# A four-layer decoder trunk: the order of the out projection's blocks, the place of two transposes, and the banks of the last product

## The chip, the core and the metric

The kernel runs on one core of a Trainium2 chip. The core has a matrix engine (TensorE, "PE" in the profile; "PEld" is its weight load), a vector engine (VectorE, "DVE"), a scalar engine (ScalarE, "ACT"), a general engine (GpSimd, "POOL") and a queue engine that issues most transfers (SyncE, "SP"). Each engine executes its own instructions in order, and an instruction that waits holds up everything behind it on that engine. The metric is the device time of one execution in microseconds; lower is better. The time before is the median of three runs, 1155.24 us (1154.94 to 1155.57).

## What is computed

The reference is a decoder trunk of four layers over 256 tokens of width 1024, in float32. Each layer is a token mixer and a squared-ReLU MLP, each behind an RMS norm, on one residual stream:

```
for i in range(4):
    a = rms_norm(h, attn_norm_g[i])
    y = mixer[i % 3](a)            # 0 differential attention, 1 MoBA, 2 sliding window
    h = h + y                      # y ends with  o @ w_out
    b = rms_norm(h, mlp_norm_g[i])
    h = h + square(max(b @ w_up[i], 0)) @ w_down[i]
return rms_norm(h, final_norm_g)
```

So layers 0 and 3 use differential attention (8 heads, each the difference of two attentions of width 64, with a normalized result of width 128), layer 1 MoBA and layer 2 sliding-window attention. The width of the MLP is 4096.

## The kernel before

All products are made from split operands: a float32 matrix is taken as a high part that fits the fast matmul format and a low part, and a product is the sum of high by high, high by low and low by high. `mm3` (L271 to L273) issues the three as matmuls of their own; `block_step` (L599, L600) joins two of them into one matmul of 512 columns.

The weights arrive in 185 pieces of 128 x 2048 (1 MB each) through SyncE's queue (L66) into four buffers called raw. `stage` splits each piece in two halves of 1024 columns: ScalarE copies the high part (whi, L80), VectorE subtracts it from the raw one to get the low part (wlo, L81). whi and wlo have three buffers each (LOOK + 1). `take` fetches and stages pieces ahead of their use, so a new piece goes into the buffer of the piece three places before it, and its copy waits until TensorE has read that one for the last time.

The residual stream is kept transposed, as four tiles hT0 to hT3 of 128 x 512; each holds two blocks d of 128 rows by 256 tokens (d = 0 to 7, block d in tile d // 2, half d % 2). `into` (L611 to L621) takes a finished product of block d out of its PSUM bank: VectorE adds it to hT (L618), then `norm_part` makes the operand of the next product, hg: its high part on ScalarE (L228), its low part on VectorE (L229). After the second block of a tile `norm_sum` squares it on ScalarE (L233) and adds up on VectorE (L238).

`out_proj_all` is the out projection of layers 0, 2 and 3. Its four weight pieces are four groups g of 256 of its 1024 inputs. In each g it goes over the eight blocks d; two blocks share a PSUM bank (p_d0 to p_d3), each block takes six matmuls in a g (two inputs of `mm3`), and in the last g each block goes to `into` when it is done. The MLP's `up_proj` follows (p_up, banks of another pool), whose first group goes over the eight blocks of hg in their order. Layer 1 has `out_proj`, which is not touched.

The mixer of layers 0 and 3 makes six projections in turn (`proj`, p_in: two of queries and keys, one of values, and the same again) and works on the heads in between. The list `plan` says which step of which head stands midway of each projection (even entries) or after it (odd ones): QK splits queries and keys, SC makes scores, TR transposes the weights, AV multiplies by the values and normalizes, OUT transposes the normalized result of a pair of heads (o, L404) on TensorE (p_o, L409) and splits it into the operand oo (L411, L412).

The last MLP product of layer 3 is `down_out`: two column halves c of 512 by two row halves t of 128 tokens, each in a bank p_last; res holds the residual stream in rows. `close` (L698) adds a finished bank to res on VectorE and squares it on ScalarE (L700); `finish` (L706 to L719) makes the reciprocal root and writes the rows out. For the last bank (c = 1, t = 1) the last weight piece is taken by halves of 256 columns, so that the first half is closed while the second is multiplied.

At the start WARM matmuls of a tile of ones (p_warm, L133) run while the first input arrives; each is executed as two passes.

What order the instructions have on each engine is not the source's alone: a scheduler that builds the program places them by its own estimate of times, within the dependencies. Dependencies through PSUM are kept by bank: a matmul into one half of a bank waits for a read of the other half.

## Time and profile before

| | before |
|---|---|
| median of three runs | 1155.24 us |
| lowest and highest | 1154.94, 1155.57 us |
| the profiled execution's own time | 1155.61 us |
| its span, first to last instruction | 1153.7 us |
| TensorE busy | 1140.0 us (99% of the span) |
| VectorE busy | 824.2 us (71%) |
| ScalarE busy | 672.1 us (58%) |
| mean granted TensorE clock | 0.998 of full |
| mean rate of the transfers | 172 GB/s |

The page of the profile shows one execution. A row of its timeline begins with the start and the duration in us, then the engine, the line of the kernel, the operation, the tiles as out<-in and the shape; a bracket gives the idle time of the engine before it and what ended that. Matmuls are pipelined, so one may show 0.28 us where the next starts 0.12 us later: the step from start to start is what counts. The chain that ended last is followed back from the last instruction to what released each step.

### The profile page before, as it was taken

What the parts mean: (1) busy time and instruction counts of PE and PEld (TensorE: products, weight loads), DVE (VectorE), ACT (ScalarE), POOL (GpSimd) and SP (SyncE); (2) the same over time, 40 slices, a digit from 0 to 9 for tenths busy, and PEclk for the clock granted to TensorE, in tenths of its full rate; (3) what the DMA queues carried; (4) which work ended last, traced back from release to release, by engine and by line L of the source; (5) the groups of instructions that cost most, each with busy time, mean ns of one, the idle gap of its engine ahead of it and who ended that gap; (6) DMA issues with size and microseconds to landing.
All of it is one profiled execution on the core that took longest, in us unless ns stands there. A gap on an engine that the chain in (4) does not pass through costs nothing.

```text
span 1153.7 us, 17107 instructions
## 1 busy us (share of the span) xinstructions
PE 1140.0 (99%) x6558; PEld 987.4 (86%) x6558; DVE 824.2 (71%) x1631; ACT 672.1 (58%) x1239; POOL 11.5 (1%) x39
## 2 busy tenths in 40 slices
PE   9999999999999999999999999999999999999997
PEld 7788888888887888888899888888888889888886
DVE  7987877656666698776568787775567787777453
ACT  6876655544476765654447866654447676665342
POOL 1000000000000000000000000000000000000000
PEclk9999999999999999999999999999999999999999
DMA  8543455555543355555564245555553444554551
GB/s 320 201 139 118 157 208 187 195 202 182 183 146 135 121 182 187 199 198 182 183 211 141 76 147 200 201 183 183 186 199 131 151 148 145 191 201 166 186 179 36
DMA packets 30608, 198.66 MB, mean 172 GB/s; under 512 B 3520, under 2 KB 5184, under 8 KB 7360
## 3 DMA queue, kind: packets, MB, share of 16 engines
q1 hardware_dynamic: 30240, 197.06, 49.5%
q8 instruction: 51, 0.84, 0.3%
q10 hardware_dynamic: 288, 0.52, 0.1%
q14 instruction: 29, 0.24, 0.1%
HBM read 196.52 MB, written 1.05 MB: 171 GB/s over the span
## 4 chain that ended last, share of the span: by engine, by line
PE 92%; DVE 5%; DMA 1%; ACT 1%; issue 1%; SPq 0%; DVEq 0%; ACTq 0%
PE p_up L599 20%; PE p_in L296 16%; PE p_down L599 15%; PE p_up L600 11%; PE p_down L600 8%; PE p_last L271 2%; PE p_last L273 2%; PE p_last L272 2%; DVE wlo L81 2%; PE p_t L351 1%; PE p_d L273 1%; PE p_d L271 1%; PE p_d L272 1%; PE p_av L434 1%; PE p_s L271 1%; DMA raw<-in_weights 1%
## 5 line engine op out<-in xcount | busy, mean ns | idle before, releaser
L81 DVE TENSOR_TENSOR wlo<-raw,whi 128x1024 fp32r<-128x1024 f32 (+1 forms) x374 | 447.2, 1210 | 202.0 <-ACT whi L80 201.3
L80 ACT ACTIVATE whi<-raw 128x1024 fp32r<-128x1024 f32 (+1 forms) x374 | 384.7, 1046 | 207.4 <-issue 111.0
L599 PE MATMUL p_up<-hg,whi 128*128 128x512 f32 x1024 | 356.8, 393 | 0.5 <-DVE hg L229 0.2
L600 PE MATMUL p_up<-hg,wlo 128*128 128x256 f32 x1024 | 285.5, 280 | 0.0
L599 PE MATMUL p_down<-uu,whi 128*128 128x512 f32 x768 | 266.4, 391 | 0.0
L599 PEld LDWEIGHTS p_up<-hg,whi 128*128 128x128 f32 x1024 | 191.4, 187 | 42.7 <-DVE hg L229 0.7
L600 PE MATMUL p_down<-uu,wlo 128*128 128x256 f32 x768 | 215.0, 280 | 0.0
L296 PE MATMUL p_in<-whi,hg 128*128 128x512 f32 (+1 forms) x736 | 213.2, 372 | 0.2 <-ACT whi L80 0.2
L600 PEld LDWEIGHTS p_up<-hg,wlo 128*128 128x128 f32 x1024 | 193.5, 189 | 0.5
L599 PEld LDWEIGHTS p_down<-uu,whi 128*128 128x128 f32 x768 | 143.6, 187 | 31.5
L296 PEld LDWEIGHTS p_in<-whi,hg 128*128 128x128 f32 x736 | 132.0, 189 | 24.3 <-issue 1.2
L600 PEld LDWEIGHTS p_down<-uu,wlo 128*128 128x128 f32 x768 | 145.2, 189 | 0.0
L296 PE MATMUL p_in<-wlo,hg 128*128 128x512 f32 (+1 forms) x368 | 130.3, 368 | 0.5 <-DVE wlo L81 0.5
L672 ACT ACTIVATE uu<-u 128x512 fp32r<-128x512 f32 x64 | 40.6, 634 | 71.0 <-DVE u L670 71.0
L296 PEld LDWEIGHTS p_in<-wlo,hg 128*128 128x128 f32 x368 | 68.8, 189 | 12.6 <-DVE wlo L81 1.8
L605 ACT ACTIVATE cross<-p_up 128x256 f32<-128x256 f32 x128 | 48.1, 376 | 39.4 <-PE p_up L600 33.9
L228 ACT ACTIVATE hg<-hT,gn 128x256 fp32r<-128x256 f32 x64 | 31.7, 504 | 65.4 <-DVE hT L618 65.2
L336 ACT ACTIVATE e<-ns,nm 128x128 f32<-128x128 f32 (+1 forms) x128 | 56.9, 448 | 9.5 <-DVE nm L333 9.3
L673 DVE TENSOR_TENSOR uu<-u,uu 128x512 fp32r<-128x512 f32 x64 | 44.2, 691 | 21.5 <-ACT uu L672 21.5
L271 PE MATMUL p_d<-oo,whi 128*128 128x256 f32 x192 | 55.7, 290 | 0.0
L272 PE MATMUL p_d<-oo,whi 128*128 128x256 f32 x192 | 54.7, 285 | 0.0
L606 DVE TENSOR_TENSOR relu<-p_up,cross 128x256 f32<-128x256 f32 x128 | 53.6, 419 | 1.6 <-ACT cross L605 1.2
(182 smaller groups left out, 1265.1 us busy)
## 6 DMA issues: line engine op xcount, KB each, us to landing
raw<-in_weights SPq DMA_DIRECT2D x181, 1024.0 KB, 4.9
raw<-in_weights SPq DMA_DIRECT2D x8, 256.0 KB, 4.7
raw<-in_weights SPq DMA_DIRECT2D x4, 512.0 KB, 8.1
hT<-in_xT SPq DMA_DIRECT2D x8, 128.0 KB, 4.7
bias<-in_swa_row SPq DMA_DIRECT2D x1, 512.0 KB, 4.2
grow<-in_fng SPq DMA_DIRECT2D x1, 512.0 KB, 3.4
out<-res SPq DMA_DIRECT2D x4, 128.0 KB, 2.1
out<-res ACTq DMA_DIRECT2D x2, 256.0 KB, 2.2
```

What stands on the lines that cost most here:

```text
L80: A.activation(hi[:, s], raw[:, s], AF.Copy)
L81: V.tensor_tensor(lo[:, s], raw[:, s], f(hi[:, s]), op=OP.subtract)
L271: T.matmul(out, lh, rh, start=start, stop=False, **kw)
L272: T.matmul(out, lh, rl, start=False, stop=False, **kw)
L296: T.matmul(out[t], n.both[k // 2][:, k % 2, x, P * t:P * t + P], r3(kb)(parts[k // kb][w])[:, k % kb, :], start=fresh, stop=k == 7 and x + ...
L336: A.activation(e[:, s], ns[:, s], AF.Exp, bias=nm[:, t:t + 1], scale=-1.0, accum_out=l[:, t:t + 1])
L599: T.matmul(r3(2)(p), hi, x, start=start, stop=False, skip_group_check=True)
L600: T.matmul(p[:, :S], lo, x[:, 0], start=False, stop=stop, skip_group_check=True)
L605: A.activation(cross, p[:, S:], AF.Copy)
L606: V.tensor_tensor(out, p[:, :S], cross, op=OP.add)
L672: A.activation(both[:, :, 0], r3(2)(u), AF.Copy)
L673: V.tensor_tensor(both[:, :, 1], r3(2)(u), f(both[:, :, 0]), op=OP.subtract)
```

## The change

It has four parts. WARM is 10 instead of 11. In the mixer's plan, OUT(0) and OUT(1) each stand half a projection later: after the second half of projections 4 and 5 (counted from 0) and no longer midway of them. In `out_proj_all` each group takes the blocks 0, 2, 4, 6 and then 1, 3, 5, 7: the first block of each bank, then the second. In `down_out` the last bank's eight pieces are divided: the first four go to the old bank, which is closed by itself over all 512 columns (one VectorE operation more, without a square); the last four go to two banks of their own of 256 columns, each closed by itself.

```diff
-WARM = 11
+WARM = 10
...
-                    [(TR, 2), (AV, 0)], [(TR, 3), (AV, 1)], [(AV, 2), (QK, 2), (OUT, 0), (SC, 4)], [(AV, 3), (SC, 5)],
-                    [(TR, 4), (QK, 3), (OUT, 1), (SC, 6)], [(TR, 5), (SC, 7)],
+                    [(TR, 2), (AV, 0)], [(TR, 3), (AV, 1)], [(AV, 2), (QK, 2), (SC, 4)],
+                    [(OUT, 0), (AV, 3), (SC, 5)], [(TR, 4), (QK, 3), (SC, 6)], [(OUT, 1), (TR, 5), (SC, 7)],
...
-            for d in range(8):
+            for d in (0, 2, 4, 6, 1, 3, 5, 7):
...
-        def close(t, bank, c, part, first, width):
-
+        def close(t, p, c, part, first=0):
+
+            width = p.shape[-1]
             y = res[t][:, 512 * c + first:512 * c + first + width]
-            V.scalar_tensor_tensor(y, bank[:, first:first + width], factor[:, t:t + 1], y, op0=OP.mult, op1=OP.add)
-            sq = sb.tile([P, 512], F32, tag="relu", name="sq")
-            A.activation(sq[:, :width], y, AF.Square, accum_out=ss[:, part, t:t + 1])
+            V.scalar_tensor_tensor(y, p, factor[:, t:t + 1], y, op0=OP.mult, op1=OP.add)
+            if part is not None:
+                sq = sb.tile([P, 512], F32, tag="relu", name="sq")
+                A.activation(sq[:, :width], y, AF.Square, accum_out=ss[:, part, t:t + 1])
...
-            def last(t, ks, cols=slice(0, 512)):
+            def last(t, ks, p=None, first=0, alone=False):
+                p = banks[t] if p is None else p
+                cols = slice(first, first + p.shape[-1])
                 for q, k in ks:
                     hi, lo = parts[q]
                     u, s = us[4 * q + k], slice(P * t, P * t + P)
-                    mm3(banks[t][:, cols], u[:, 0, s], u[:, 1, s], hi[:, k, cols], lo[:, k, cols],
-                        q + k == 0, q + k == 10, skip_group_check=True)
+                    mm3(p, u[:, 0, s], u[:, 1, s], hi[:, k, cols], lo[:, k, cols],
+                        (q, k) == (ks[0] if alone else (0, 0)), (q, k) == ks[-1] and k == 3 and q > 5,
+                        skip_group_check=True)
...
                 finish(0, 1)
+
                 last(1, ends[:4])
+                close(1, banks[1], 1, None)
                 for h in range(2):
-                    last(1, ends[4:], slice(256 * h, 256 * h + 256))
-                    close(1, banks[1], 1, 1 + h, 256 * h, 256)
+                    p = bank("acc", "p_last")[:, :256]
+                    last(1, ends[4:], p, 256 * h, True)
+                    close(1, p, 1, 1 + h, 256 * h)
                     if h == 0:
                         sofar(1, [1])
                 finish(1, 2)
```

More of the change, by code (lines that the diff above doesn't have):

```diff
@@ L745, in down_out @@
             last(0, ends)
-            close(0, banks[0], c, c, 0, 512)
+            close(0, banks[0], c, c)
             if c == 0:
                 last(1, ends)
-                close(1, banks[1], 0, 0, 0, 512)
+                close(1, banks[1], 0, 0)
                 for t in range(NT):
```

## The prediction

> **What bounds the kernel now.** I read the page first (span, busy times, the chain that ended last), then the list of waits by engine, then the timeline around the four edited places.

> ```profile
> span 1153.7 us, 17107 instructions
> PE 1140.0 (99%) x6558; PEld 987.4 (86%) x6558; DVE 824.2 (71%) x1631; ACT 672.1 (58%) x1239; POOL 11.5 (1%) x39
> PE 92%; DVE 5%; DMA 1%; ACT 1%; issue 1%; SPq 0%; DVEq 0%; ACTq 0%
> ```

> From the list of waits (engine, line, releaser: us in total, times, longest):

> ```profile
> PE p_o L409 <- DVE o L404: 2.4, 6, 0.5
> ...
> PE p_up L599 <- DVE hg L229: 0.2, 1, 0.2
> ```

> TensorE works for 1140.0 of 1153.7 us and makes 92% of the chain. So work on the other engines costs nothing until TensorE waits for it, and a hole in TensorE's row goes into the time in full. The change removes almost no TensorE work, hence the question at each edit is which holes close and which open. The p_o waits (2.4 us) and one wait of p_last (below) are what could be won. The rest of the profiled time, 1155.61 us, lies around the span. The median of the runs is 1155.24, 0.37 below the profiled one; I sum differences and add them to the median.

> **The out projection (layers 0, 2 and 3), the costly edit.** In source the blocks come 0, 2, 4, 6 and then 1, 3, 5, 7. No matmul is added. But the scheduler had taken the first halves of the banks ahead already: the compiled order of both kernels has the same 30 p_d matmuls of the last quarter, then three p_up, then 18 p_d for the second halves of p_d1 to p_d3. What the edit does is to change when the second halves of hg are made. Timeline of before, layer 0 (start us, us, engine, line, operation), TensorE:

> ```profile
> 120.96 0.28 PE L273 MATMUL p_d<-oo,wlo 128*128 128x256 f32 x1
> 121.36 0.50 PE L599 MATMUL p_up<-hg,whi 128*128 128x512 f32 x1
> 121.70 0.28 PE L600 MATMUL p_up<-hg,wlo 128*128 128x256 f32 x1
> 121.81 0.39 PE L599 MATMUL p_up<-hg,whi 128*128 128x512 f32 x1
> 122.05 0.28 PE L600 MATMUL p_up<-hg,wlo 128*128 128x256 f32 x1
> 122.16 0.40 PE L599 MATMUL p_up<-hg,whi 128*128 128x512 f32 x1
> 122.40 0.28 PE L271 MATMUL p_d<-oo,whi 128*128 128x256 f32 x1
> ...
> 124.44 0.28 PE L273 MATMUL p_d<-oo,wlo 128*128 128x256 f32 x1
> 124.56 0.40 PE L599 MATMUL p_up<-hg,whi 128*128 128x512 f32 x1
> ```

> No hole from 121.36 on. ScalarE and VectorE in the same stretch:

> ```profile
> 117.38 2.01 ACT L80 ACTIVATE whi<-raw 128x1024 fp32r<-128x1024 f32 x2 [3.75 <-PE p_d L272]
> 119.30 0.49 ACT L228 ACTIVATE hg<-hT,gn 128x256 fp32r<-128x256 f32 x1
> 121.68 0.51 ACT L228 ACTIVATE hg<-hT,gn 128x256 fp32r<-128x256 f32 x1 [1.89 <-DVE hT L618]
> ...
> 122.62 1.89 ACT L228 ACTIVATE hg<-hT,gn 128x256 fp32r<-128x256 f32 x4
> ...
> 125.34 1.05 ACT L80 ACTIVATE whi<-raw 128x1024 fp32r<-128x1024 f32 x1
> ```

> ```profile
> 118.56 2.35 DVE L81 TENSOR_TENSOR wlo<-raw,whi 128x1024 fp32r<-128x1024 f32 x2
> 120.83 0.48 DVE L229 SCALAR_TENSOR_TENSOR hg<-hT,gn,hg 128x256 fp32r<-128x256 f32 x1
> 121.22 1.08 DVE L618 TENSOR_TENSOR hT<-p_d,hT 128x256 f32<-128x256 f32 x3
> 122.22 0.48 DVE L229 SCALAR_TENSOR_TENSOR hg<-hT,gn,hg 128x256 fp32r<-128x256 f32 x1
> ```

> Before, ScalarE makes the second half of hg0 at 121.68 and VectorE its low part at 122.22, over 2 us before TensorE asks; the copy of the next weights (whi18) comes after the hg's, at 125.34. The compiled order of the changed kernel is another (line numbers of before; the wait of each instruction in brackets):

> ```
> ACT L228 hg3<-hT3,gn 128x256            [waits DVE]      (first half)
>     L80  whi18<-raw18 128x1024          [waits DMA, PE]
>     L228 hg0<-hT0,gn 128x256            [waits DVE]      (second half)
> DVE L618 hT3<-p_d3,hT3 128x256          [waits PE]       (second half)
>     L81  wlo18<-raw18,whi18 128x1024    [waits DMA, ACT]
>     L229 hg0<-hT0,gn,hg0 128x256        [waits ACT]      (second half)
> PE  18 p_d (odd blocks), 5 p_up with the first half of hg0, then
>     L599 p_up<-hg0,whi16 128x512        [waits DVE]      (second half)
> ```

> whi has three buffers, so whi18 goes where whi15 was, and whi15 is read by the last quarter of the out projection up to the 17th of these 18 p_d. The whole second half of hg now queues on ScalarE behind a copy that waits for TensorE, and on VectorE behind the subtract that waits for that copy. Step by step, layer 0:
> - Start of p_up: the chain up to it (0.42 hT, two wlo, hg0's low part 120.83 to 121.31) keeps its order, so 121.36 again. d = 1 to be issued after three p_up: 122.05. 18 p_d at (124.56 − 122.40) / 18 = 0.12 each: until 124.21. Five p_up by the rows 121.70 to 122.40 (0.24 wide, 0.11 narrow): TensorE asks at 125.01.
> - The 17th p_d starts at 122.05 + 16 × 0.12 = 123.97 and ends 0.28 later. whi18's first half starts at 124.29 and ends at 125.34 (1.05 of the row). hg0's second half starts one copy step later, (119.30 − 117.38) / 2 = 0.96, at 125.25, so it is no longer what is late: VectorE's wlo18 starts at 125.38, and after one subtract step, (120.83 − 118.56) / 2 = 1.14, the low part of hg0 starts at 126.52 and ends at 127.00. p_up goes on at 127.05.
> - Hole 127.05 − 125.01 = 2.04, and the first matmul after a wait takes 0.34 to the next where a running one takes 0.24 (121.36 and 121.81): **+2.15 us**. The other second halves follow on VectorE at 0.4 to 0.5 us each, and TensorE needs one only every four pairs of matmuls (1.4 us), so there is one hole and no second.

> Layer 2 has the same compiled order; layer 3 too, but for one thing: the transposes of the residual (p_res) now fill the hole.

> ```profile
> 672.67 0.47 PE L599 MATMUL p_up<-hg,whi 128*128 128x512 f32 x1 [0.22 <-DVE hg L229]
> ```

> ```profile
> 964.95 0.50 PE L599 MATMUL p_up<-hg,whi 128*128 128x512 f32 x1
> ```

> ```profile
> L793 PE MATMUL p_res<-ident,hT x16: 272/272/273, 978.9 to 980.5; 128*128 128x128 f32 x16
> ```

> Layer 2: **+2.15** (a hole until 672.67 + 5.69 = 678.36). Layer 3: 16 transposes at 1.6 / 15 = 0.11 take 1.74 of the 2.04: **+0.40** with the restart. Their copies on ScalarE (L796) now stand ahead of the first reads of p_up; with some 5 us of matmuls before these are wanted I count 0, and 0.5 at worst.
> Bounds of one hole: from below 1.0 (if the low part of hg0 stood ahead of the subtract, 1.14 less), from above 2.5 (one more hg step of 0.48 ahead). I take the compiled order's 2.15.

> **Results turned half a group later (layers 0 and 3).** OUT(0) had no hole before it. OUT(1) and OUT(2):

> ```profile
> 85.42 0.40 PE L296 MATMUL p_in<-wlo,hg 128*128 128x512 f32 x1
> 86.13 0.63 PE L409 MATMUL p_o<-ident,o 128*128 128x128 f32 x4 [0.31 <-DVE o L404]
> ```

> ```profile
> 103.69 0.52 PE L409 MATMUL p_o<-ident,o 128*128 128x128 f32 x3 [0.36 <-DVE o L404]
> ```

> A p_in steps at 0.23, so p_o at 86.13 stands 0.48 late; moved half a product later it waits for nothing. But TensorE then reaches the scores of head 6 by 0.48 + 0.45 (the transposes) sooner, while ScalarE's copies of their keys move up by the p_o copy only (0.69): 0.24 comes back. Then comes the wait before OUT(2), whose chain runs over ScalarE's squares and VectorE and not over TensorE alone. So 0 to 0.24 is left per layer; I take 0.14, or **−0.28** for two. Ends: −0.48, and +0.3 if the scores wait longer.

> **Last piece in banks of its own.** TensorE, VectorE, and the 512 wide form of the close (ns min/median/max):

> ```profile
> 1143.96 0.28 PE L273 MATMUL p_last<-whi,uu 128*128 128x256 f32 x1
> 1144.82 0.39 PE L271 MATMUL p_last<-whi,uu 128*128 128x256 f32 x1 [0.58 <-DVE res L698]
> 1145.04 0.28 PE L272 MATMUL p_last<-wlo,uu 128*128 128x256 f32 x1
> ...
> 1146.23 0.28 PE L273 MATMUL p_last<-whi,uu 128*128 128x256 f32 x1
> ```

> ```profile
> 1144.28 0.48 DVE L698 SCALAR_TENSOR_TENSOR res<-p_last,factor,res 128x256 f32<-128x256 f32 x1
> ...
> 1146.55 0.48 DVE L698 SCALAR_TENSOR_TENSOR res<-p_last,factor,res 128x256 f32<-128x256 f32 x1 [1.05 <-PE p_last L273]
> ```

> ```profile
> L698 DVE SCALAR_TENSOR_TENSOR res<-p_last,factor,res x5: 484/747/750, 1096.6 to 1146.5; 128x512 f32<-128x512 f32 x3, 128x256 f32<-128x256 f32 x2
> ```

> The second half waits until VectorE has read the first half's bank. In a bank of its own it starts at 1144.08, and its 12 matmuls at 0.12 start their last at 1145.39 instead of 1146.23: **−0.84**, which goes through to the end, because the close, the square, the root and the two writes behind it are a chain. The added close (0.75) falls into VectorE's finish of the first rows and pushes the first half's close from 1144.28 to some 1145.03, ended at 1145.51; the last close can start at 1145.71, so it is covered by 0.2. Without that cover the gain shrinks by what exceeds it: ends −0.84 and −0.4. One scalar operation (L725) moves behind the last close, under ScalarE's square: 0.

> **Warm-up, 11 to 10.**

> ```profile
> L133 PE MATMUL p_warm<-ones x22: 354/421/582, 1.0 to 5.6; 128*128 128x128 f32 x22
> ```

> ```profile
> 5.71 1.34 PE L296 MATMUL p_in<-whi,hg 128*128 128x512 f32 x4
> ```

> ```profile
> 5.05 0.49 ACT L228 ACTIVATE hg<-hT,gn 128x256 fp32r<-128x256 f32 x1
> ```

> Two passes of 0.21 fewer, but the first p_in needs hg (ended 5.54), so it starts 0.1 sooner at most, and the next pieces of input arrive when they did: **0**.

> **Sum:** 2.15 + 2.15 + 0.40 − 0.28 − 0.84 + 0 = +3.58; 1155.61 becomes 1159.2 in the profiled execution, and the median 1155.24 becomes 1158.8 (+0.3%).

> **Rivals.**
> 1. No hole in the out projection, and faster. Place: whi18's copy. It would decide where the copy starts by 122.5 instead of 124.29, so each long hole shrinks under 0.35; then −0.28 − 0.84 is left: 1154.1. For it: only the order of the queues, no work, is against the holes. Against it: the copy writes the buffer that 17 of the 18 p_d still read, and before it never started ahead of them either. 0.05.
> 2. Within the bound: all p_o waits (2.4 us) go, the later starts leaving slack for each: 4.70 − 2.4 − 0.84 = +1.5, 1156.7. For it: all six are the same wait. Against it: OUT(2) and OUT(3), which end the mixer, are not moved, so four of the six stay. 0.11 with all other shorter holes.
> 3. TensorE's clock falls in a 2 us hole. Price by rows: p_warm's passes at the start step at 4.6 / 21 = 0.22, those of p_res at 0.11, and it took from 1.0 to 5.7, 4.7 us, until p_in ran at speed; that again loses 2.1 us a hole, 4.1 for two: 1162.9. For it: nothing seen but the slow start. Against it: the longest hole of before after the start, 0.6 us, was followed by steps at the full 0.12, though none was as long. 0.04. [...]

> **How the numbers follow.** The forecast holds 0.80: 1158.8, by itself 1157.6 (one hole a half shorter) to 1160.4 (mixers +0.3 each, which is 0.9 worse, p_res copies +0.5, rounded up for the runs' 0.3). The range reaches to case 2 and leaves out 1 and 3: 1156.5 to 1160.4. What a measurement of this kernel can tell from no change is 0.2%, 2.3 us. Faster by more 0.05 (case 1 and better), same 0.11, slower 0.84.

> **What would show it.** Right: in layers 0 and 2 a p_up that waits about 2 us for VectorE's hg, behind a wlo that follows ScalarE's whi copy waiting for p_d; in layer 3 p_res there and a wait under 0.5; no wait at the last product's second half, whose matmuls run 12 in a row; p_o at OUT(1) with no wait. Wrong: whi copied before the odd p_d end, or hg's second halves ahead of it; the matmuls after the hole stepping at more than 0.24; a new wait on the added close.

## The result and the profile after

The changed kernel takes 1159.46 us (median of seven), 1.0039 times the kernel before (95% interval 1.0028 to 1.0049; 1155.03 us on the same chip). The prediction was 1158.8 us, between 1156.5 and 1160.4. In one of the seven, the one that was profiled, TensorE's clock stood at 0.556 throughout (1888.74 us), so it is left out of the ratio (the other six have a median of 1159.2), and the profile below is that of a second run of the same kernel (1157.34 us, the shortest of its five; median of the five 1158.92).

From the page of the profile after:

```profile
span 1155.3 us, 17105 instructions
PE 1138.9 (99%) x6556; PEld 984.5 (85%) x6556; DVE 824.8 (71%) x1632; ACT 670.7 (58%) x1239; POOL 11.4 (1%) x39
PE 92%; DVE 3%; ACT 2%; DMA 1%; issue 1%; SPq 0%; DVEq 0%; ACTq 0%
```

TensorE's list of waits after (us in total, times, longest):

```profile
PE p_up L599 <- DVE hg L229: 4.7, 5, 1.9
PE p_o L409 <- DVE o L404: 1.6, 4, 0.5
```

The wait of p_up for hg is 4.7 us where it was 0.2, the waits of p_o are four and no longer six, and the wait of p_last is gone from the list. The 4.7 us are two waits of 1.86, the holes, and three of 0.30 to 0.40 at the first p_up of a layer. Those three cost next to nothing: they were 0.12 to 0.22 before, and the first p_up stands as far behind the work ahead of it as without the new order, to 0.05 us. So it is by chance that the 4.7 equals the prediction's sum for the holes. The same places in the timeline after. TensorE in layers 0, 2 and 3:

```profile
123.52 0.28 PE L600 MATMUL p_up<-hg,wlo 128*128 128x256 f32 x1
125.66 0.50 PE L599 MATMUL p_up<-hg,whi 128*128 128x512 f32 x1 [1.86 <-DVE hg L229]
...
676.84 0.28 PE L600 MATMUL p_up<-hg,wlo 128*128 128x256 f32 x1
678.98 0.50 PE L599 MATMUL p_up<-hg,whi 128*128 128x512 f32 x1 [1.86 <-DVE hg L229]
...
970.59 1.91 PE L801 MATMUL p_res<-ident,hT 128*128 128x128 f32 x16
972.60 0.50 PE L599 MATMUL p_up<-hg,whi 128*128 128x512 f32 x1
```

ScalarE and VectorE in layer 0:

```profile
120.27 1.31 ACT L228 ACTIVATE hg<-hT,gn 128x256 fp32r<-128x256 f32 x3 [1.89 <-DVE hT L618]
122.89 1.06 ACT L80 ACTIVATE whi<-raw 128x1024 fp32r<-128x1024 f32 x1 [1.30 <-PE p_d L272]
123.85 0.49 ACT L228 ACTIVATE hg<-hT,gn 128x256 fp32r<-128x256 f32 x1
```

```profile
123.98 1.23 DVE L81 TENSOR_TENSOR wlo<-raw,whi 128x1024 fp32r<-128x1024 f32 x1 [0.55 <-ACT whi L80]
125.12 0.88 DVE L229 SCALAR_TENSOR_TENSOR hg<-hT,gn,hg 128x256 fp32r<-128x256 f32 x2
```

Everything here lies 1.40 us earlier than in the prediction's working (125.66 for 127.05), but in the order and at the distances that it has: ScalarE idles 1.30 us for p_d, then copies whi; VectorE waits for whi, then wlo, then hg's low part; TensorE stands from 123.63 (one narrow step after 123.52) to 125.66. In layer 3 the transposes p_res stand in the hole.

The step from one kernel to the other, read as the difference of start times of the same matmul:

| stretch | term of the prediction | measured | from which two profiles |
|---|---|---|---|
| hole, layer 0 | +2.15 | +2.03 | the change without and with the new block order |
| hole, layer 2 | +2.15 | +2.05 | the same |
| hole, layer 3 | +0.40 | +0.47 | the same |
| mixer, layers 0 and 3 | −0.14 each | −0.70, −0.73 | before, and the change without the block order |
| last product | −0.84 | −0.83 | the same |
| warm-up, until layer 0's scores | 0 | −0.05 | the same |
| sum | +3.58 | +2.24 | |

By this sum the time would be 1155.0 + 2.2 = 1157.3 us, and that is what the shortest executions of the changed kernel take (1156.72, 1157.16 and 1157.34 in three runs). The medians of those runs are 1159.46, 1158.92 and 1158.31. So between one and two of the four us are in none of the rows above, and they differ from execution to execution: those of the kernel before lay between 1154.55 and 1156.10 in 60 executions, those of the changed kernel between 1156.72 and 1162.13 in 18. What this is was the open question for the experiments.

### The profile page after: what moved, and what is told of

Same layout as the page of the kernel before. It is cut to its first block, busy times and chain, and to the rows that moved or that the text cites. A ratio compares the mean times of both kernels' runs of the same rounds, so it can differ in the third digit from the quotient of the medians.

```text
span 1886.8 us, 17105 instructions
## 1 busy us (share of the span) xinstructions
PE 1876.0 (99%) x6556; PEld 1320.5 (70%) x6556; DVE 835.7 (44%) x1632; ACT 676.5 (36%) x1239; POOL 11.4 (1%) x39
## 3 DMA queue, kind: packets, MB, share of 16 engines
HBM read 196.52 MB, written 1.05 MB: 105 GB/s over the span
## 4 chain that ended last, share of the span: by engine, by line
PE 99%; DVE 0%; ACT 0%; DMA 0%; issue 0%; DVEq 0%; SPq 0%
PE p_up L599 21%; PE p_in L296 20%; PE p_down L599 16%; PE p_up L600 10%; PE p_down L600 8%; PE p_last L272 3%; PE p_last L273 3%; PE p_last L271 3%; PE p_d L273 2%; PE p_d L272 2%; PE p_d L271 2%; PE p_t L351 1%; PE p_av L434 1%; PE p_qk L459 1%; PE p_s L271 1%; PE p_s L273 1%
## 5 line engine op out<-in xcount | busy, mean ns | idle before, releaser
L81 DVE TENSOR_TENSOR wlo<-raw,whi 128x1024 fp32r<-128x1024 f32 (+1 forms) x374 | 446.8, 1209 | 637.8 <-ACT whi L80 637.1
L80 ACT ACTIVATE whi<-raw 128x1024 fp32r<-128x1024 f32 (+1 forms) x374 | 383.3, 1043 | 681.2 <-issue 276.3
L599 PE MATMUL p_up<-hg,whi 128*128 128x512 f32 x1024 | 569.9, 575 | 2.5 <-DVE hg L229 2.5
L599 PE MATMUL p_down<-uu,whi 128*128 128x512 f32 x768 | 426.1, 574 | 0.0
L600 PE MATMUL p_up<-hg,wlo 128*128 128x256 f32 x1024 | 394.0, 385 | 0.0
L599 PEld LDWEIGHTS p_up<-hg,whi 128*128 128x128 f32 x1024 | 225.0, 220 | 162.5 <-issue 71.9
L296 PE MATMUL p_in<-whi,hg 128*128 128x512 f32 (+1 forms) x736 | 325.7, 539 | 0.1
L600 PE MATMUL p_down<-uu,wlo 128*128 128x256 f32 x768 | 295.4, 385 | 0.0
L599 PEld LDWEIGHTS p_down<-uu,whi 128*128 128x128 f32 x768 | 168.2, 219 | 121.2 <-issue 58.6
L600 PEld LDWEIGHTS p_up<-hg,wlo 128*128 128x128 f32 x1024 | 230.6, 225 | 7.4 <-issue 0.4
L296 PEld LDWEIGHTS p_in<-whi,hg 128*128 128x128 f32 x736 | 162.0, 230 | 92.0 <-issue 52.0
L296 PE MATMUL p_in<-wlo,hg 128*128 128x512 f32 (+1 forms) x368 | 189.7, 533 | 0.0
L600 PEld LDWEIGHTS p_down<-uu,wlo 128*128 128x128 f32 x768 | 172.4, 224 | 5.1
L296 PEld LDWEIGHTS p_in<-wlo,hg 128*128 128x128 f32 x368 | 86.5, 237 | 44.6 <-issue 24.6
L272 PE MATMUL p_last<-wlo,uu 128*128 128x512 f32 (+1 forms) x132 | 74.6, 565 | 0.0
L273 PE MATMUL p_last<-whi,uu 128*128 128x512 f32 (+1 forms) x132 | 74.6, 565 | 0.0
L271 PE MATMUL p_d<-oo,whi 128*128 128x256 f32 x192 | 74.5, 388 | 0.0
L271 PE MATMUL p_last<-whi,uu 128*128 128x512 f32 (+1 forms) x132 | 74.3, 563 | 0.0
L273 PE MATMUL p_d<-oo,wlo 128*128 128x256 f32 x192 | 74.0, 386 | 0.0
L272 PE MATMUL p_d<-oo,whi 128*128 128x256 f32 x192 | 74.0, 386 | 0.0
```

Source lines behind the costliest of these rows:

```text
L80: A.activation(hi[:, s], raw[:, s], AF.Copy)
L81: V.tensor_tensor(lo[:, s], raw[:, s], f(hi[:, s]), op=OP.subtract)
L271: T.matmul(out, lh, rh, start=start, stop=False, **kw)
L272: T.matmul(out, lh, rl, start=False, stop=False, **kw)
L273: T.matmul(out, ll, rh, start=False, stop=stop, **kw)
L296: T.matmul(out[t], n.both[k // 2][:, k % 2, x, P * t:P * t + P], r3(kb)(parts[k // kb][w])[:, k % kb, :], start=fresh, stop=k == 7 and x + ...
```

## The experiments

**The changed kernel again.** No edit.

> The changed kernel once more, for a profile at the usual clock. Theory A (two holes of about 2 us before the second half of hg, layers 0 and 2, and 0.4 us in layer 3; clock unharmed): in each profile p_up waits 2.0 to 2.2 us for VectorE's hg near 125 and near 676 us, mean granted clock 0.998 as before, 1158.8 us, and the executions lie as close together as those of the kernel before (under 1 us). Rival B (the hole lets TensorE's clock fall in some executions): the same holes, but the executions spread over several us, the longer ones at a lower mean clock, and in their profiles matmuls right behind a hole step at 0.46 us where they step at 0.23 elsewhere. Rival C (the loss is somewhere else): no hole of over 1 us near 125 or 676 us.

Measured: 1157.34, 1158.83, 1161.64, 1161.08, 1158.92 us, at mean granted clocks of 0.999, 0.997, 0.996, 0.997, 0.997 (the mean is 0.999 at most in every run: in the profile of the kernel before the last 4.4 us of the span, behind the last matmul, stand at 0.50). The holes are there, so rival C falls. The spread and the clocks speak for B, but the profile, of the shortest execution, shows no slow step behind a hole.

**Without the new block order.**

```diff
-            for d in (0, 2, 4, 6, 1, 3, 5, 7):
+            for d in range(8):
```

> The change without the new order of the out projection's blocks (warm-up, plan and last banks stay). Theory A and rival B alike: no hole before the second half of hg, so what is left is the last banks' -0.84 and the mixers' -0.28: 1153.9 us, clock 0.998, and close executions. Rival C (the loss comes from one of the other parts): above 1157 us.

Measured: 1152.76 us (1152.26 to 1153.56), 0.9982 times the kernel before (0.9973 to 0.9991). From its list of waits:

```profile
PE p_up L599 <- DVE hg L229: 0.2, 1, 0.2
```

No hole; the loss is all the block order's. The other three parts gain 2.1 us and not 1.1: TensorE reaches layer 0's up projection 0.75 us and layer 3's 1.52 us earlier than before. This is the version that beats both kernels.

**The new block order alone.**

```diff
-            for d in range(8):
+            for d in (0, 2, 4, 6, 1, 3, 5, 7):
```

> The new order of blocks alone in the kernel before. Theory A: +2.15 +2.15 +0.40 = +4.7, 1159.8 us, executions within 1 us of each other. Rival B: at least the same, spread over several us with the clock. Rival C: within 1 us of the kernel before.

Measured: 1159.73 us (1159.12 to 1161.28), as theory A has it; its list of waits begins with the same row as that of the change (p_up for hg, 4.7 us, 5 times). Four of the five executions lie within 0.7 us, and all five have clocks of 0.998.

**The last banks alone.** The edits of `down_out` in the kernel before.

> The last banks alone in the kernel before. Theory: the wait of 0.6 us before the second half is gone, 12 matmuls run on in a row, last matmul 0.84 us earlier and the end with it: 1154.2 us. Rival (the added close delays the first half's close so that the last close waits for VectorE): under 0.5 us gained, and the last close starts over 0.1 us after the last matmul's end.

Measured: 1154.24 us (1154.10 to 1154.58), ratio 0.9993 (0.9984 to 1.0002), against an expected 1154.2. The interval of the ratio reaches past 1, but all eleven executions are as short as the shortest of 21 beside them of the kernel before (1154.58) or shorter, and its profile has the last 12 matmuls in a row and 0.51 us before the last close. In the profile of the changed kernel VectorE at that place (L699 is the close, and 512 wide the added one):

```profile
1145.48 0.74 DVE L699 SCALAR_TENSOR_TENSOR res<-p_last,factor,res 128x512 f32<-128x512 f32 x1
1146.14 0.15 DVE L715 SCALAR_TENSOR_TENSOR fr<-nw,fr 128x1 f32<-128x1 f32 x1
1146.33 0.88 DVE L720 SCALAR_TENSOR_TENSOR res<-res,fr,grow 128x256 f32<-128x256 f32 x2
1147.13 0.48 DVE L699 SCALAR_TENSOR_TENSOR res<-p_last,factor,res 128x256 f32<-128x256 f32 x1
1148.12 0.48 DVE L699 SCALAR_TENSOR_TENSOR res<-p_last,factor,res 128x256 f32<-128x256 f32 x1 [0.51 <-PE p_last L273]
```

VectorE has half a microsecond to spare before the last close, which waits for TensorE: the added 0.74 is covered.

**The mixers' plan alone.**

> The mixers' plan alone in the kernel before. As the prediction had it: 0.14 a layer, 1154.7 us. By the trace of the change without the new block order, which reached the out projection 0.70 us earlier in layer 0 and 0.75 in layer 3: 1153.5 us. Rival (that gain was the warm-up's): 1154.9 us.

Measured: 1153.70 us (1153.32 to 1154.03), ratio 0.9989 (0.9979 to 0.9998). The gain is the plan's, not the warm-up's: it has the 1.3 us without the shorter warm-up. By the medians beside them the two parts, −0.7 and −1.3, make −1.9 of the −2.1 of the version without the block order, which leaves 0.2 at most for the warm-up, less than the spread of any of the three.

**Work in the holes.** The changed kernel, with transposes in layers 0 and 2 like those of p_res in layer 3 (results not used):

```diff
                     V.reciprocal(held["row"], x)
+                    for j in range(4 if i != 1 else 0):
+                        p = bank("acc", "p_fill")
+                        for t in range(4):
+                            T.transpose(p[:, P * t:P * t + P], hT[j][:, P * t:P * t + P], ident)
```

> The changed kernel with 16 transposes of the residual stream added in layers 0 and 2 (their results are not used); in the compiled order they stand where TensorE waited, as the residual's own transposes do in layer 3. The stall of the chain stays, but TensorE works through 1.7 of its 2.0 us. Rival B (the hole makes the clock fall in some executions): no clock lost, executions within 1 us of each other near the shortest of the changed kernel, 1157.3 us, mean clock 0.998 or more in each. Theory A (the clock is not concerned, the spread has another cause): 1158.9 us with the same spread of 4 us.

Measured: 1158.97 us (1157.79 to 1159.59), no clock under 0.998. TensorE is as late as ever, but not idle (timeline, layer 0):

```profile
124.00 1.91 PE L795 MATMUL p_fill<-ident,hT 128*128 128x128 f32 x16
126.02 0.50 PE L599 MATMUL p_up<-hg,whi 128*128 128x512 f32 x1
```

The median alone would not tell A from B, so this kernel was run once more, beside the changed one:

> The kernel with transposes in the holes once more, beside the changed kernel on the same chip. Rival B: no execution with a mean clock under 0.998, spread under 2 us, longest under 1160 us. Theory A: the same clocks and the same spread as the changed kernel's beside it.

Measured: 1157.82 us (1157.17 to 1159.80), again no clock under 0.998. Over both, 13 executions have a median of 1157.87 us, the changed kernel's 18 one of 1158.88; beside each other on one chip the medians are 1157.82 and 1158.31. So useless work in the holes does not make the kernel longer; that it makes it shorter is likely, but times that spread so much do not settle it. The clocks part the two kernels: none of 13 executions is under 0.998, of the changed kernel 10 of 18. The times are still spread over 2.6 us, and rival B had asked for under 2, so the clock is not all that spreads them.

**The holes doubled.**

```diff
-            stage()
+            stage(2048 if len(staged) in (18, 107) else 1024)
```

> The changed kernel with the weights that stand ahead of hg's second halves (piece 18 in layer 0, piece 107 in layer 2) split in one copy and one subtract of 2048 columns and not in two of 1024: the copy is longer by 0.95 and the subtract by 1.14 us, so each of the two holes is 4.1 and not 2.0 us. Theory A: 1158.9 + 4.2 = 1163.1 us. Rival B: the clock falls in almost every execution at both holes, some 1.7 us and more each on top of the shortest 1157.3 + 4.2: 1165 us or more, the mean clock 0.996 or less, and in the profile matmuls behind the holes that step at 0.46 us.

Measured: 1165.55 us (1163.99 to 1166.83), clocks 0.993 to 0.996: rival B's number. Timeline behind the first hole, and windows (start:end, length, busy time and count of PE, PEld, DVE, ACT and POOL, then the granted clock, the share of the DMA engines and GB/s):

```profile
127.67 0.79 PE L599 MATMUL p_up<-hg,whi 128*128 128x512 f32 x1 [3.78 <-DVE hg L229]
128.26 0.42 PE L600 MATMUL p_up<-hg,wlo 128*128 128x256 f32 x1
128.48 0.63 PE L599 MATMUL p_up<-hg,whi 128*128 128x512 f32 x1
128.91 0.41 PE L600 MATMUL p_up<-hg,wlo 128*128 128x256 f32 x1
129.12 0.63 PE L599 MATMUL p_up<-hg,whi 128*128 128x512 f32 x1
```

```profile
126.00:128.00 2.00, 0.33 (x1) 0.33 (x2) 2.00 (x4) 1.53 (x4) 0.00 (x0) 0.86 0.00 0
128.00:130.00 2.00, 2.00 (x7) 1.71 (x7) 2.00 (x5) 1.15 (x2) 0.00 (x0) 0.50 0.79 233
130.00:132.00 2.00, 2.00 (x10) 1.67 (x10) 1.12 (x3) 0.00 (x0) 0.00 (x0) 0.79 0.69 291
132.00:134.00 2.00, 2.00 (x13) 1.74 (x12) 0.00 (x0) 0.03 (x1) 0.00 (x0) 1.00 0.04 8
```

Behind a hole of 3.8 us idle a pair of p_up takes 0.64 us and not 0.35, the granted clock is 0.50, and it is back at 1.00 some 3 us after the restart (behind the second hole, over 5 us: the window from 684 to 690 us has 0.50 throughout). So behind both holes of this length the clock fell.

**The warm-up of before.** `WARM = 11` in the changed kernel.

> The changed kernel with the warm-up of before (11). Theory (the warm-up is worth nothing, TensorE waits for the first input anyway): same times as the changed kernel, 1158.9 us with a spread of some 4 us. [...]

Measured: 1157.99 us (1157.34 to 1160.26), four of six executions under 1158.3 us. And the other way round, the block order with the shorter warm-up:

> The new order of blocks with the shorter warm-up, without the plan and the last banks. Theory A: as the order of blocks alone, 1159.7 us. Rival B: holes as in the changed kernel, so 1159.4 us where the clock holds and 1.5 to 2 us more for each fall, mean clocks between 0.996 and 0.999. If the shorter warm-up decides whether it falls, most executions are above 1160.5 us, where the order of blocks alone had one in five.

Measured: 1161.05 us (1159.51 to 1161.47), three of five above 1160.5. In both pairs the longer warm-up is ahead, by about 1 us, which is within the spread of the kernels without it. In the kernels without holes the shorter warm-up costs nothing. This stays open.

**The changed kernel a third time.**

> The changed kernel a third time, for a profile of an execution that is not its shortest. Rival B (a hole of 2 us lets the clock fall in some executions): in an execution of 1158.5 us or more one of the stretches behind the holes (126 to 131 or 678 to 683 us) shows a granted clock between 0.5 and 1, its pairs of p_up matmuls step at 0.64 us in place of 0.35, and it costs some 1.5 to 2 us a hole; executions again from 1157.3 to 1162 us. Theory A: the granted clock is 1.00 behind both holes whatever the time.

Measured: 1158.31 us (1156.72 to 1160.05), two of seven at a clock of 0.997. The profiled execution took 1160.05, and it is not what rival B expected: the clock is 1.00 behind both holes, as theory A has it, but A names no cause for its length. Its span is 2.85 us longer than that of the profile shown above. Of this, 1.9 come in the first 20 us, where a weight piece lands late:

```profile
16.18 0.63 ACT L80 ACTIVATE whi<-raw 128x512 fp32r<-128x512 f32 x1 [2.27 <-DMA raw<-in_weights]
```

Half a microsecond is won back in small steps in layers 1 and 3, and 1.48 come in layer 3's up projection, spread evenly over it. Of seven rows in a row from each the first three and the last, first the profile shown above, then this one:

```profile
999.69 0.39 PE L599 MATMUL p_up<-hg,whi 128*128 128x512 f32 x1
999.92 0.27 PE L600 MATMUL p_up<-hg,wlo 128*128 128x256 f32 x1
1000.03 0.40 PE L599 MATMUL p_up<-hg,whi 128*128 128x512 f32 x1
...
1000.72 0.40 PE L599 MATMUL p_up<-hg,whi 128*128 128x512 f32 x1
```

```profile
999.92 0.40 PE L599 MATMUL p_up<-hg,whi 128*128 128x512 f32 x1
1000.16 0.28 PE L600 MATMUL p_up<-hg,wlo 128*128 128x256 f32 x1
1000.28 0.40 PE L599 MATMUL p_up<-hg,whi 128*128 128x512 f32 x1
...
1000.98 0.40 PE L599 MATMUL p_up<-hg,whi 128*128 128x512 f32 x1
```

Three pairs take 1.03 us in the one and 1.06 in the other, at a granted clock of 1.00 in both and with no wait. Over the 77.6 us from its 65th matmul to its last that is 1.48 us, and the profile of the block order with the shorter warm-up has the very same 1.48 in the same layer. In none of the profiles without holes does an up projection of the four layers differ from that of the kernel before by more than 0.1 us.

**Sixteen holes.** To have many in one profile, the change without the block order, with a wait put in behind four groups of each up projection:

```diff
             us += [both[:, b] for b in range(2)]
+            if g in (3, 6, 9, 12):
+                h = n.both[0][:, 0]
+                V.scalar_tensor_tensor(h, r3(2)(ps_up[1]), 0.0, f(h), op0=OP.mult, op1=OP.add)
```

> Sixteen separate holes in one execution: the change without the new block order (1152.8 us, no hole in its MLPs), and after groups 3, 6, 9 and 12 of each up projection VectorE rewrites the first part of hg0 with itself plus zero times the group's last product, so that TensorE has to wait for a chain cross (0.38), relu (0.42), rewrite (0.75) and the handovers, 1.7 to 2.1 us, 16 us apart. The values stay as they are. Theory A (holes of this length never let the clock fall): the granted clock is 1.00 behind all 16, pairs of p_up step at 0.35 us behind each, 1152.8 + 16 x 1.9 = 1183 us, mean clock 0.998. Rival B (they do in some cases): behind some of the 16 the granted clock is under 0.9 and pairs step at 0.64 us, mean clock 0.99 or less, and 1.5 to 2 us more for each. Rival D (what spreads the times is TensorE's rhythm after a restart, seen as 0.353 us a pair in place of 0.347 in layer 3's up projection in two profiles of the new block order): the steps differ from hole to hole, 0.347 behind some and 0.353 behind others, at a granted clock of 1.00.

Measured: 1242.64 us (1236.09 to 1243.79), clocks 0.970 to 0.976. The holes came out longer than meant, 3.31 us idle each, because a weight copy and its subtract got between (as in the change itself). Two of the sixteen, and the windows behind them:

```profile
148.06 0.47 PE L599 MATMUL p_up<-hg,whi 128*128 128x512 f32 x1 [3.31 <-DVE hg L677]
148.37 0.30 PE L600 MATMUL p_up<-hg,wlo 128*128 128x256 f32 x1
148.48 0.61 PE L599 MATMUL p_up<-hg,whi 128*128 128x512 f32 x1
148.89 0.41 PE L600 MATMUL p_up<-hg,wlo 128*128 128x256 f32 x1
...
214.78 0.47 PE L599 MATMUL p_up<-hg,whi 128*128 128x512 f32 x1 [3.31 <-DVE hg L677]
215.09 0.28 PE L600 MATMUL p_up<-hg,wlo 128*128 128x256 f32 x1
215.20 0.40 PE L599 MATMUL p_up<-hg,whi 128*128 128x512 f32 x1
215.44 0.28 PE L600 MATMUL p_up<-hg,wlo 128*128 128x256 f32 x1
```

```profile
148.20:148.45 0.25, 0.25 (x2) 0.20 (x3) 0.25 (x2) 0.00 (x0) 0.00 (x0) 1.00 0.00 0
148.50:148.90 0.40, 0.40 (x4) 0.30 (x3) 0.40 (x2) 0.36 (x1) 0.00 (x0) 0.50 0.00 0
149.00:151.00 2.00, 2.00 (x8) 1.71 (x7) 1.24 (x2) 0.17 (x1) 0.00 (x0) 0.50 0.39 57
151.60:151.90 0.30, 0.30 (x3) 0.30 (x2) 0.00 (x0) 0.00 (x0) 0.00 (x0) 0.50 0.73 273
151.92:152.20 0.28, 0.28 (x3) 0.24 (x3) 0.00 (x0) 0.00 (x0) 0.00 (x0) 1.00 1.03 380
...
214.00:216.00 2.00, 1.22 (x7) 1.11 (x8) 2.00 (x4) 0.63 (x1) 0.00 (x0) 1.00 0.04 12
```

Sixteen holes of one length, and two things happen behind them. Behind 12 the granted clock is 0.50, and a pair of p_up takes 0.64 us, until 3.1 to 6.3 us after the restart, which costs 1.5 to 2.9 us each (the next 40 matmuls against 6.95 us for 40 at the full pace); behind four it stays at 1.00. And behind each the steps settle at one of two paces, eight matmuls in 1.39 us or in 1.41 to 1.42, eight holes each, and keep it until the next hole. Rivals B and D both hold at this length; theory A does not.

Windows around three more of the holes:

```profile
192.00:195.00 3.00, 1.85 (x6) 1.59 (x7) 3.00 (x6) 0.66 (x2) 0.00 (x0) 0.64 0.02 5
...
1055.00:1058.00 3.00, 2.25 (x9) 1.99 (x10) 2.94 (x5) 0.63 (x1) 0.00 (x0) 0.74 0.03 5
```

```profile
462.00:464.00 2.00, 0.81 (x3) 0.75 (x4) 2.00 (x5) 0.40 (x2) 0.00 (x0) 0.63 0.52 217
...
469.00:471.00 2.00, 2.00 (x13) 1.80 (x12) 0.42 (x1) 0.12 (x1) 0.00 (x0) 0.91 0.00 0
```

With 0.50 and 1.00 as the two clocks, these means put the falls at 192.84, 462.52 and 1056.44 us and one rise at 469.36, each to about 0.03 us; the busy time of TensorE in the same rows gives the ends of the holes, 193.15, 463.19 and 1055.75. The first hole's fall is at 148.49 and its rise at 151.91, 3.42 us later; the other four changes lie 13, 92, 266 and 94 steps of 3.413 us behind 148.49, within the same 0.03 us. In time cut into such steps, the hole that ends at 148.06 leaves TensorE idle for 87% of one step, and these three for 88, 77 and 80%: behind all four the clock fell. The one that ends at 214.78 is divided, 55% of one step and 42% of the next, and behind it the clock stayed at 1.00. So these five holes of one length differ in their place against the steps, and the clock stayed behind the one with the smallest share of a step; what share is enough, five holes do not tell. A hole of the changed kernel, 1.86 us idle by the same count, can fill no more than 55% of a step (1.86 of 3.413 us), and behind the ten that were profiled the clock was 1.00.

## Why the prediction was right

**The holes** (+4.70 predicted, +4.55 measured): the step of the prediction that carries it all. The compiled order named what would be late and what it waits for, and the durations of the rows of before gave the sizes: predicted hole 2.04, measured 2.03 in layer 0. Shifted by the 1.40 us that TensorE is earlier, whi (124.29), wlo (125.38) and hg's low part (126.52) start to 0.01 us where the working had them. That hg on ScalarE would no longer be what is late, but wlo on VectorE, is right too. Layer 3's 0.47 bears out that the transposes fill its hole. No second hole followed, and the copies of p_res delayed nothing.

**The mixers** (−0.28 predicted, −1.43 measured, outside the ends of −0.48 and +0.3 that the prediction gave): the step that failed. Of the 0.48 that the wait of p_o costs I let 0.24 "come back" at the scores of head 6, and took 0.14 of the rest. In the profile of the change without the block order a wait of only 0.11 appears at the scores, where ScalarE's second copy of the keys starts at 87.08 for 87.51 before; TensorE is 0.50 earlier at the out projection's first product and 0.70 at its end. So all of the 0.48 stays, and some 0.2 more in small steps, of which 0.09 is the wait before OUT(2) (0.27 for 0.36). The whole wait in each of the two layers, −0.96, should have been the value taken, since nothing in the rows of before showed the keys to be late; where the other 0.1 in each layer comes from is open.

**The last product** (−0.84, measured −0.83) with its cover (0.2 predicted, 0.51 measured), and **the warm-up** (0, measured −0.05 without holes) came out as worked out.

**Rival 3, the clock**: its chance of 0.04 was too small. Two of its figures are off by a little: 21 steps at 0.22 in place of 0.11 lose 2.3 us and not 2.1, and the longest hole of before after the start is 0.65 us (p_qk) and not 0.6. In 10 of 18 executions of the changed kernel the mean clock is under 0.998. That is at least 5.8 us at half the clock (an estimate, from 0.0025 of 1157 us lost at half the pace), more than a profile spends so at its end: 4.4 us in that of the kernel before, 5.2 in that of the last banks alone. The medians of the two groups are 1159.2 and 1157.7 us. Over all kernels with these holes it is 14 of 34 executions; over those with the holes filled 0 of 13; over the 33 of the versions without holes 0, and over 60 of the kernel before 0. The price is of the size of what the sixteen holes show, 1.5 to 2.9 us. What no profile shows is the fall itself behind a hole of 2 us: in the ten such holes that were profiled (five profiles, two each) the clock was 1.00. So the fall is shown behind holes of 3.3 us and more, and for the 2 us holes it is inferred from the mean clocks and from the filled kernel; at 1.86 us they fill 55% of a step of 3.413 us at most, about as much as the hole that ends at 214.78 does, and behind that one the clock stayed. So this stays open.

**What this makes of the whole.** With the mixers sized as measured, the prediction's sum would have been 1157.5 us. The measured 1159.46 is near 1158.8 because an underrated gain of 1.1 us and an underrated loss of 1 to 2 us stand against each other, which is luck. The sign and the cause are the prediction's, the last microsecond is not. How that loss divides between clock, pace (1.48 in two profiles out of eight with the new block order) and the late first weights (up to 1.9 in one profile) can't be told for an execution without a profile of it.

## What to carry to other kernels

When an order is changed in source and a scheduler places the instructions, look at where the copies for later work now stand in each engine's queue: here nothing was added, and a weight copy that waits for TensorE got ahead of an operand that TensorE waits for. An idle stretch of the bounding engine cost its length here (2.03 and 2.05 us) and can cost more: behind 3.3 us and longer it took the clock in 14 of 18 holes here, and the kernels with holes of 2 us spread over several us. So work that is needed anyway belongs in it (with p_res in the hole, layer 3 lost 0.47 us). And of a change in four parts undo one at a time: three of these gain 2.1 us together, and the fourth loses 6.
